# Three more chunks of the up projection by seven products, and more low parts of weights by DMA

## The chip, the cores and the metric

One core of one Trainium2 chip runs the whole program. The metric is device time in microseconds, the median of several runs. TensorE does the matmuls, VectorE (DVE) and ScalarE (ACT) the elementwise work, GpSimd (POOL) mostly issues DMAs that add into their destination, and SyncE (SP) issues the loads.

## The reference

A trunk of two residual layers over 512 tokens of width 1024, in float32. Layer 0 mixes tokens by gated linear attention, layer 1 by grouped-query softmax attention. After each mixer comes a gated MLP with a width-3 convolution over tokens:

```python
def conv_ffn(h, w_up, w_conv, b_conv, w_down):
    u = h @ w_up                      # 1024 -> 2 * 2816
    u = conv3(u, w_conv) + b_conv     # along tokens, per feature
    val, gate = jnp.split(u, 2, axis=-1)
    return (jax.nn.silu(gate) * val) @ w_down
for i in range(DEPTH):
    ...
    x = x + conv_ffn(rmsnorm(x, norm_ffn[i]), ffn_w_up[i], ffn_w_conv[i], ffn_b_conv[i], ffn_w_down[i])
```

The change touches the up projection of this MLP in both layers. (`conv3` stands for the reference's depthwise convolution.)

## The kernel before

**Two halves for one float32.** Every operand of a matmul is kept as a high part and a low part (`wh`, `wl` for weights; `nh`, `nl` and `xt` for activations), and a product is three matmuls: high by high, high by low, low by high. The high part is a copy by ScalarE that rounds. The low part is either a subtraction on VectorE (`split`, L320), or `low_dma`: ScalarE writes the negated rounded value (L272), and a DMA from POOL's queue (`flush`, L308) adds the unrounded value onto it, read from SBUF or, where `home` is given, from the weights in DRAM.

**Chunks.** The 2816 features of the MLP are 22 chunks `m` of 128, each with a value tile (t = 0) and a gate tile (t = 1) of 128 features x 512 tokens. There are two ways to compute a chunk:

- `plain_up(m)`: two tiles, each 8 steps of 3 matmuls with 512 columns, 48 matmuls (L482 to L484, output `up`). The weights are two pieces of 128 x 1024.
- `seven_up(m)`, for `m` in `SEVEN`: the two tiles by two halves of the tokens as a 2 x 2 block product, by seven block products in place of eight (the scheme of Strassen and Winograd). Each product has 4 pairs of 3 matmuls with 256 columns, 84 in all (L1074, output `r`). The weights are four pieces: two as loaded, a sum of quarters (h = 2, made with L293 and L294), and a half-size difference (h = 3). Between products ScalarE doubles a block (`twice`, L1129) or copies one (L1095, L1102), and VectorE adds (L1132); product 4 can only begin when the copy L1095 is done, product 6 when `twice` of product 1 is.

**Order.** `Weights.todo` is a list of the pieces in order of use; each call of `W.piece` makes pieces ahead of use (six in the wide phase from chunk 1 to 19, four after that) and loads three further ones through SP. Raw loads share a ring of five buffers of 128 x 1024 (`raw`), from which the sum tile is taken too; a buffer is free when the last reader of its contents has finished, a DMA included.

After chunk 9 and chunk 17 (`DOWN_AFTER`) a part of the down projection runs, four steps `n` of 84 narrow matmuls, again by seven products, each adding its result to x in DRAM through POOL's queue. Its first product is placed inside the chunk ahead (between the tiles of a plain chunk), as the first product of chunk m + 1 is placed inside a seven-product chunk m (`begin_up`), so that a doubling by ScalarE is covered by other matmuls. In `add_ffn` one swap in the list of pieces goes with it: the first piece of the down part comes ahead of the plain chunk's second piece.

Before, `SEVEN` holds 6, 7, 8, 10 to 13, 15, 16 and 18 to 21; chunks 0 to 5, 9, 14 and 17 are plain. `LOW_0`, `LOW_1` and `LOW_2` name the seven-product chunks whose piece h = 0, 1 or 2 gets its low part by DMA: chunks 7 and 8 for h = 0, none for the others. A piece h = 0 is read again from DRAM for that, a piece h = 2 from the sum tile in SBUF.

The engines' orders are not written by hand here: a scheduler orders each engine's instructions by priority and readiness at build time, and each engine then works through its list in order.

Of the kernel before, what the change touches and what calls it, by code (L numbers as in the profile page):

```python
# [66 lines left out]
DOWN_AFTER = {9: 0, 17: 1}  # L67


SEVEN = (6, 7, 8, 10, 11, 12, 13, 15, 16, 18, 19, 20, 21)  # L70
UPA = 3
PA = 4
LOADS = 3
# [1 line left out]
INPUT_AT = {2: (0, 1), 3: (2,), 4: (3,)}  # L75
Q_DMA = ()
UP_DMA = (1, 2, 5)
LOW_0 = (7, 8)
LOW_1 = ()
LOW_2 = ()  # L80
STRIP_0 = ()
STRIP_2 = ()
NR = 5
# [17 lines left out]
def hybrid_encoder_kernel(  # L101
# [39 lines left out]
    def bank(tag, n):  # L141
        return pp.tile([P, S], F32, tag=tag, bufs=PS[tag], name=nm(n))
# [4 lines left out]
    def big(dt, n):  # L147
        return pair("g", 22, dt, n)

    def tmp(tag, n, w=S):  # L150
        return sp.tile([P, w], F32, tag=tag, bufs={"u": 3, "t": 5, "sq": 3}[tag], name=nm(n))
# [24 lines left out]
    class Weights:  # L176
# [98 lines left out]
        def summed(self, src, i, h):  # L275
# [20 lines left out]
            r = self.strip[id(src), i][h]  # L296
            low = (LOW_0, LOW_1, LOW_2) if any(src is a for a in up) else (STRIP_0, (), STRIP_2)
            if i in low[h]:
# [41 lines left out]
    W = Weights()  # L340
# [3 lines left out]
    def add_up(layer, chunks):  # L344
        for m in chunks:
            W.add(up[layer], (m,), 4 if m in SEVEN else 2)
            if m in SEVEN and m - 1 not in SEVEN and m - 1 not in DOWN_AFTER:
                W.todo[-5:-3] = W.todo[-4], W.todo[-5]

    def add_ffn(layer):  # L350
        first = 0
        for m, part in DOWN_AFTER.items():
            add_up(layer, range(first, m + 1))
            W.add(down_w[layer], range(part * NQ, (part + 1) * NQ), 4)
            at = len(W.todo) - 4 * NQ - 1
            W.todo[at : at + 2] = W.todo[at + 1], W.todo[at]
            first = m + 1
        add_up(layer, range(first, FC))
        W.add(down_w[layer], range(NPART * NQ, down_w[layer].shape[0]))
# [9 lines left out]
    for a in qk_order[:2] + [w_av] + qk_order[2:] + [w_aout]:  # L369
        W.add(a)  # L370
    add_ffn(1)
    W.by_dma += [(w_kq, KQ_DMA)] + [(a, 1) for a in qk_order + [w_av]] + [(w_aout, 2)]

# [121 lines left out]
    def feature_tile(*a):  # L495
        for last in feature_steps(*a):
            pass
        return last
# [518 lines left out]
    def ffn(layer, norm, cw, nxt):  # L1017
        w_dn = down_w[layer]

        ahead = {(m + i // 2, i % 2): n for m in DOWN_AFTER for i, n in ((-1, 2), (0, 2), (1, 5))}  # L1020
        ahead.update({(m - 1 + i // 2, i % 2): n for m in SEVEN for i, n in ((-1, 2), (0, 2), (1, 5))})
        plain = {}
        down = []
# [5 lines left out]
        def rescale():  # L1029

            for p in range(KC // 2):
                xr = big(F32, "xr")
                for i in range(2):
                    c = 2 * p + i
                    dve.scalar_tensor_tensor(xr[:, i * S : (i + 1) * S], x[c], norm.weight(c), norm.R, ALU.mult, ALU.mult)
                hi, lo = big(F32R, "nh"), big(F32R, "nl")
                W.low_dma(hi, lo, xr)
                scaled.append(xr)
                fresh.extend((hi[:, i * S : (i + 1) * S], lo[:, i * S : (i + 1) * S]) for i in range(2))

        def plain_up(m):

            pss = []
            for t in range(2):
                ps = bank("s" if t else "acc", "up")
                feature_tile(*W.half(up[layer], 2 * m + t, max(UPAW if W.wide else UPA, ahead.get((m, t), 1))), norm.hl if m < SWITCH else fresh, ps)
                pss.append(ps)
                if t == 0 and m not in DOWN_AFTER:
                    begin_up(m + 1)
                if t == 0 and m in DOWN_AFTER:  # L1050
                    down.append(down_part(DOWN_AFTER[m], m))
                    next(down[-1])
                if m == 0 and t == 0:
                    norm.tokens()
                elif m == 0:
                    norm.rows()
                    rescale()
            for t, ps in enumerate(pss):
                u = ps
                if m < SWITCH:  # L1060
                    u = tmp("u", "u")
                    dve.tensor_tensor(u, ps, norm.R, ALU.mult)
                yield t, u

        def product(pieces, src, strip, pairs, i, dst, start):
            h, o = PLACE[i]
            if h not in pieces:
                pieces[h] = W.piece(src, strip, h, PAW if W.wide else PA)
            wh, wl = pieces[h]
            for j, p in enumerate(pairs):  # L1070
                sl = slice(o + j * P, o + (j + 1) * P)
                mh, ml = p[i]
                for a, (w, m) in enumerate(((wh, mh), (wh, ml), (wl, mh))):
                    mm(dst, w[:, sl], m, start=start and j == 0 and a == 0, stop=j == len(pairs) - 1 and a == 2,  # L1074
                       skip_group_check=True)
            W.flush()

        def begin_up(m):
            if m in SEVEN:
                begun.append(seven_up(m))  # L1080
                next(begun[-1])

        def seven_up(m):

            pieces = {}
            go = lambda *a: product(pieces, up[layer], m, inputs, *a)
            r = bank("pt", "r1")[:, :H]
            go(1, r, True)
            both = bank("acc", "r")
            r1, r2 = both[:, :H], both[:, H:]  # L1090
            twice(both, r)
            yield
            go(6, r2, False)
            r3 = bank("s", "r3")
            act.activation(r3[:, :H], r2, AF.Copy)  # L1095
            r4 = bank("pt", "r4")[:, :H]
            go(7, r4, True)
            d = tmp("u", "u")
            twice(d, r4)
            go(4, r3[:, :H], False)  # L1100
            go(5, r2, False)
            act.activation(r3[:, H:], r2, AF.Copy)  # L1102
            add_seven(d, r3, r4)
            yield 1, d
            begin_up(m + 1)
            go(2, r1, False)
            go(3, r2, False)
            yield 0, both

        def act_up(m):  # L1110

            res = {}
            for t, u in begun.pop(0) if m in SEVEN else plain_up(m):
                cc = ((layer * 2 + t) * FC + m) * 4
# [12 lines left out]
        def twice(d, r4):  # L1127
            two = lambda a: a.rearrange("p (o t) -> p o t", t=H)
            act.activation(two(d), two(r4).to_broadcast([P, 2, H]), AF.Copy)  # L1129

        def add_seven(d, r3, r4):
            dve.tensor_tensor(d, d, r3, ALU.add)  # L1132
# [49 lines left out]
        def down_part(part, m):  # L1182

            pairs = [quads.pop(part * NQ + i) for i in range(NQ)]
            st = {}
            pieces = [{} for _ in range(NQ)]
            go = lambda n, *a: product(pieces[n], w_dn, part * NQ + n, pairs, *a)

            def begin(n):
                r = bank("pt", "r1")[:, :H]
                go(n, 1, r, True)
                st[n] = bank("acc", "r")
                twice(st[n], r)

            begin(0)
            yield
            for n in range(NQ):
                r, c, d = st[n], x_home[n][:, :S], x_home[n][:, S:]  # L1200
                r1, r2 = r[:, :H], r[:, H:]
                go(n, 6, r2, False)
                r3 = bank("s", "r3")
                act.activation(r3[:, :H], r2, AF.Copy)
                r4 = bank("pt", "r4")[:, :H]
                go(n, 7, r4, True)
                g, f = tmp("u", "g"), tmp("u", "f")
                twice(f, r4)
                go(n, 4, r3[:, :H], False)
                go(n, 5, r2, False)  # L1210
                act.activation(r3[:, H:], r2, AF.Copy)  # L1211
                add_seven(f, r3, r4)
                W.pending.append((d, f))
                if n + 1 < NQ:
                    begin(n + 1)
                else:
                    begin_up(m + 1)
                go(n, 2, r1, False)
                go(n, 3, r2, False)
                act.activation(g, r, AF.Copy)  # L1220
                W.pending.append((c, g))
# [15 lines left out]
        for m in range(FC):  # L1237
# [15 lines left out]
            else:  # L1253
                for i, y in enumerate(held):
                    t = big(F32R, "gu")
# [244 lines left out]
    ffn(0, norms[1], cw, norms[2])  # L1500
    attention(norms[2], norms[3])
    ffn(1, norms[3], cw, None)


def _layout(inputs):
# [61 lines left out]
    seven = np.stack(quarters, 1).transpose(0, 4, 3, 1, 2, 5).reshape(2, FC, P, 4 * S)  # L1567
    a["w_up"][:, list(SEVEN)] = seven[:, list(SEVEN)]
    dn = i["ffn_w_down"].reshape(2, FC, P, KC, P)
# [29 lines left out]
```

## Time and profile before

| | |
|---|---|
| median of 3 runs | 1087.22 us (1086.87 to 1087.8) |
| profiled execution, span from first to last instruction | 1085.5 us |
| what lies around that span, against the runs' median | 1.7 us |
| TensorE busy | 1077.5 us, 99% |
| VectorE busy | 888.5 us, 82% |
| ScalarE busy | 721.1 us, 66% |
| GpSimd busy | 136.7 us, 13% |
| granted TensorE clock | 1.000 |

The span is one execution's time from its first to its last instruction. A busy share is a mean over stages. Matmuls overlap: the profile's length of one (0.39 us for 512 columns, 0.28 for 256) is longer than the distance from one to the next, so distances are taken from start times.

### The profile page before, as it was taken

To read this page: it belongs to the slowest core of one execution; us is meant where nothing else is said; L and a number is where in the kernel's file an instruction comes from. 1 tells how busy PE (TensorE), PEld (TensorE's weight loads), DVE (VectorE), ACT (ScalarE), POOL (GpSimd) and SP (SyncE) were. 2 spreads that over 40 slices of the span, in tenths; PEclk is the share of its full clock that TensorE was granted. 3 is DMA by queue.
4 is the path that set the end of the run, shared out by engine and by line. 5 is a ranking of instruction groups with operands and counts; after the bars stand their busy time and mean duration, and the time that the engine had idled before them with its cause. 6 is when DMAs were issued, how large, how long until landed. Compare 5 with 4: busy or idle time off the path is not lost.

```text
span 1085.5 us, 17391 instructions
## 1 busy us (share of the span) xinstructions
PE 1077.5 (99%) x6672; PEld 966.4 (89%) x6672; DVE 888.5 (82%) x1327; ACT 721.1 (66%) x1134; POOL 136.7 (13%) x153
## 2 busy tenths in 40 slices
PE   9999999999999999999999999999999999999998
PEld 8888988888999999999988888888889999999997
DVE  7998967569898899988755588666989889998882
ACT  8679575478775676666574677656877567666660
POOL 0212112021001100010015333002110010001000
PEclk9999999999999999999999999999999999999999
DMA  8744446499545633274767475549863473227542
GB/s 301 187 126 106 122 141 215 154 207 204 127 125 127 145 120 111 77 177 121 252 149 162 127 204 164 164 158 202 206 148 124 105 166 116 100 80 157 136 175 78
DMA packets 55763, 164.52 MB, mean 152 GB/s; under 512 B 6528, under 2 KB 7040, under 8 KB 55680
## 3 DMA queue, kind: packets, MB, share of 16 engines
q1 hardware_dynamic: 36192, 112.66, 32.2%
q0 software_dynamic: 14592, 42.21, 21.7%
q10 hardware_dynamic: 4896, 8.55, 2.1%
q8 instruction: 52, 0.85, 0.3%
q14 instruction: 31, 0.25, 0.1%
HBM read 114.89 MB, written 14.68 MB: 119 GB/s over the span
## 4 chain that ended last, share of the span: by engine, by line
PE 87%; DVE 6%; ACT 3%; DMA 2%; issue 2%; POOL 0%; SPq 0%; DVEq 0%; ACTq 0%; POOLq 0%
PE r L1074 37%; PE op L535 8%; PE vg L652 7%; PE up L482 4%; PE up L483 4%; PE up L484 4%; PE dn L483 2%; PE dn L484 2%; PE dn L482 2%; PE av L509 1%; PE A L482 1%; DVE wl L320 1%; PE A L484 1%; DMA nl<-xr 1%; PE B L484 1%
## 5 line engine op out<-in xcount | busy, mean ns | idle before, releaser
L320 DVE TENSOR_TENSOR wl<-raw,wh 128x1024 fp32r<-128x1024 f32 x156 | 189.8, 1220 | 31.3 <-ACT wh L319 31.1
L319 ACT ACTIVATE wh<-raw 128x1024 fp32r<-128x1024 f32 x156 | 162.6, 1053 | 73.4 <-PE op L535 20.7
L1074 PE MATMUL r<-gu,wh 128*128 128x256 f32 x896 | 161.2, 282 | 0.0
L1074 PE MATMUL r<-xt,wh 128*128 128x256 f32 x832 | 151.1, 283 | 0.4 <-ACT r L1095 0.3
L1074 PEld LDWEIGHTS r<-gu,wh 128*128 128x128 f32 x896 | 139.3, 190 | 1.0 <-ACT r L1211 0.2
L1074 PEld LDWEIGHTS r<-xt,wh 128*128 128x128 f32 x832 | 129.2, 190 | 1.6 <-ACT r L1095 1.1
L1074 PE MATMUL r<-gu,wl 128*128 128x256 f32 x448 | 126.3, 283 | 0.0
L1074 PE MATMUL r<-xt,wl 128*128 128x256 f32 x416 | 117.2, 283 | 0.0
L1074 PE MATMUL r<-nh,wh 128*128 128x256 f32 x312 | 88.8, 285 | 0.3 <-ACT r L1102 0.3
L1074 PE MATMUL r<-nh,wl 128*128 128x256 f32 x312 | 88.2, 283 | 0.0
L1074 PE MATMUL r<-nl,wh 128*128 128x256 f32 x312 | 87.9, 282 | 0.0
L1074 PEld LDWEIGHTS r<-gu,wl 128*128 128x128 f32 x448 | 85.1, 190 | 0.0
L1074 PEld LDWEIGHTS r<-xt,wl 128*128 128x128 f32 x416 | 79.1, 190 | 0.0
L482 PE MATMUL up<-nh,wh 128*128 128x512 f32 x192 | 75.3, 392 | 0.0
L483 PE MATMUL up<-nl,wh 128*128 128x512 f32 x192 | 75.2, 392 | 0.0
L484 PE MATMUL up<-nh,wl 128*128 128x512 f32 x192 | 75.2, 392 | 0.0
L535 PE MATMUL op<-oT,wh 128*128 128x512 f32 x256 | 72.4, 393 | 0.0
L271 ACT ACTIVATE wh<-raw 128x1024 fp32r<-128x1024 f32 x36 | 38.0, 1056 | 38.2 <-PE up L483 11.5
L1074 PEld LDWEIGHTS r<-nh,wh 128*128 128x128 f32 x312 | 59.3, 190 | 2.9 <-ACT r L1102 2.6
L1074 PEld LDWEIGHTS r<-nl,wh 128*128 128x128 f32 x312 | 59.4, 190 | 0.2
L1074 PEld LDWEIGHTS r<-nh,wl 128*128 128x128 f32 x312 | 59.4, 190 | 0.0
L535 PEld LDWEIGHTS op<-oT,wh 128*128 128x128 f32 x256 | 47.4, 188 | 9.7 <-ACT oT L937 0.3
(299 smaller groups left out, 2761.6 us busy)
## 6 DMA issues: line engine op xcount, KB each, us to landing
raw<-in_w_up_dram SPq DMA_DIRECT2D x84, 512.0 KB, 4.6
raw<-in_w_down_dram SPq DMA_DIRECT2D x44, 512.0 KB, 3.7
wl<-raw POOLq DMA_DIRECT2D x20, 512.0 KB, 5.3
wl<-in_w_up_dram POOLq DMA_DIRECT2D x16, 512.0 KB, 7.8
ring<-p ACTq DMA_DIRECT2D x32, 256.0 KB, 2.6
xw<-in_xw_dram SPq DMA_DIRECT2D x8, 512.0 KB, 6.6
raw<-in_w_v_dram SPq DMA_DIRECT2D x8, 512.0 KB, 5.9
raw<-in_w_g_dram SPq DMA_DIRECT2D x8, 512.0 KB, 4.0
```

What stands on the lines that cost most here:

```text
L271: act.activation(hi, r, AF.Copy)
L319: act.activation(hi[:, sl], a, AF.Copy)
L320: dve.tensor_tensor(lo[:, sl], a, hi[:, sl].bitcast(F32), ALU.subtract)
L482: mm(ps, wh, mh, start=start, stop=False)
L483: mm(ps, wh, ml, start=False, stop=False)
L484: return mm(ps, wl, mh, start=False, stop=stop)
L509: mm(ps[j][:, :width], hl[k][i == 2][:, j * P : (j + 1) * P], (wl if i == 1 else wh)[:, sl], start=k == 0 and i == 0, stop=k == KC - 1 and ...
L535: mm(pss[ng][n], wt[:, sl], mv, start=k == late[0][0] and i == 0, stop=k == late[-1][-1] and i == 2)
L652: last = mm(ps[j], m[:, js], w[:, sl], start=i in (1, 7, 2) and p == 0 and a == 0, stop=i in (4, 2, 3) and p == 3 and a == 2, skip_group_c ...
L1074: mm(dst, w[:, sl], m, start=start and j == 0 and a == 0, stop=j == len(pairs) - 1 and a == 2, skip_group_check=True)
```

## The change

`SEVEN` becomes all chunks from 6 to 21: chunks 9, 14 and 17 of both layers are computed by seven products. What follows a first product inside a chunk is chosen in one place, `begin(m)`: a down part where `m` is in `DOWN_AFTER`, otherwise the next chunk. The swap in `add_ffn` is kept for plain chunks alone. `LOW_0` gets 11 more chunks and `LOW_2` eight, so that 19 more pieces a layer get their low part by DMA. The weights of the three chunks are laid out as quarters on the host, which the existing code does from `SEVEN`.

```diff
-SEVEN = (6, 7, 8, 10, 11, 12, 13, 15, 16, 18, 19, 20, 21)
+SEVEN = tuple(range(6, 22))
...
-LOW_0 = (7, 8)
+LOW_0 = (7, 8, 9, 11, 12, 13, 14, 15, 16, 17, 19, 20, 21)
 LOW_1 = ()
-LOW_2 = ()
+LOW_2 = (8, 9, 13, 14, 15, 16, 17, 20)
...
             at = len(W.todo) - 4 * NQ - 1
-            W.todo[at : at + 2] = W.todo[at + 1], W.todo[at]
+            if m not in SEVEN:
+                W.todo[at : at + 2] = W.todo[at + 1], W.todo[at]
...
-                if t == 0 and m not in DOWN_AFTER:
-                    begin_up(m + 1)
-                if t == 0 and m in DOWN_AFTER:
-                    down.append(down_part(DOWN_AFTER[m], m))
-                    next(down[-1])
+                if t == 0:
+                    begin(m)
...
+        def begin(m):
+            if m in DOWN_AFTER:
+                down.append(down_part(DOWN_AFTER[m], m))
+                next(down[-1])
+            else:
+                begin_up(m + 1)
...
             yield 1, d
-            begin_up(m + 1)
+            begin(m)
             go(2, r1, False)
```

## The prediction

> **What bounds the kernel now.** I read the busy times of the engines first, then the chain that ended last, in order of time, then a table by stretch for the chunks that the change touches, and last single instructions there. The page's head:
>
> ```profile
> span 1085.5 us, 17391 instructions
> ...
> PE 1077.5 (99%) x6672; PEld 966.4 (89%) x6672; DVE 888.5 (82%) x1327; ACT 721.1 (66%) x1134; POOL 136.7 (13%) x153
> ```
>
> TensorE is busy for 99% of the span; POOL's 153 pieces of work take 0.89 us each. The chain in order of time (start, length, what) shows what TensorE spends a chunk on. Here it runs from chunk 8 through down part 0 and chunks 10 to 13 into plain chunk 14 of layer 0:
>
> ```profile
> 313.55 2.90 PE r L1074 x24
> ...
> 321.25 1.45 PE r L1074 x12
> ...
> 328.18 75.90 PE r L1074 x636
> 404.77 2.98 PE r L1074 x24
> ...
> 412.53 1.43 PE r L1074 x12
> ...
> 419.54 15.78 PE r L1074 x132
> ```
>
> L1074 is the matmul of 256 columns in a seven-product piece of work. 636 of them follow one another in 75.90 us without a wait, 0.1193 us each, so a seven-product chunk (7 products x 4 pairs x 3 = 84) takes 10.02 us. The rows between these, which I left out, are 512-wide matmuls of the plain chunks 9 and 14. From 313.55 to 328.18 are 14.63 us; the 24 and 12 narrow ones take 4.35, which leaves 10.28. From 404.77 to 419.54 are 14.77, less 4.41 leaves 10.36. In each of the two stretches lie 45 of the plain chunk's 48 matmuls (three stand ahead of it), so one costs 20.64/90 = 0.2293 us and a plain chunk 11.01 us.
>
> Now the same place by stretch. The columns are busy us (and counts) of TensorE, its weight loads, VectorE, ScalarE and GpSimd, then the granted clock, the share of the DMA engines and GB/s. The stretches are chunks 10 to 13, plain 14, 15 and 16, plain 17:
>
> ```profile
> core 0: us, PE busy (x) PEld busy (x) DVE busy (x) ACT busy (x) POOL busy (x), PEclk, DMA share, GB/s
> 368.10:408.20 40.10, 40.10 (x332) 39.71 (x331) 37.81 (x51) 28.24 (x44) 0.87 (x1) 1.00 0.46 127
> 408.20:419.40 11.20, 11.20 (x57) 9.39 (x56) 11.20 (x15) 6.86 (x10) 0.00 (x0) 1.00 0.33 111
> 419.40:439.50 20.10, 20.10 (x164) 19.73 (x163) 20.10 (x31) 14.52 (x24) 0.00 (x0) 1.00 0.32 105
> 439.50:450.50 11.00, 11.00 (x55) 9.27 (x54) 10.23 (x18) 7.48 (x12) 0.00 (x0) 1.00 0.16 48
> sum 82.40, PE 82.40 PEld 78.09 DVE 79.34 ACT 57.10 POOL 0.87; mean PE 20.60 PEld 19.52 DVE 19.84 ACT 14.27 POOL 0.22
> ```
>
> TensorE binds, but VectorE is full in chunks 14 to 16 (11.20 of 11.20, 20.10 of 20.10): the plain chunks are where it catches up. ScalarE has 25 us to spare, the DMA engines more than half.
>
> **The change, part by part.** *Matmuls.* In each of two layers chunks 9, 14 and 17 go from 48 wide to 84 narrow matmuls: 11.01 - 10.02 = 0.99 us less, six times 5.9 us. All of it is on the path.
>
> *Work around them.* The prices, from the groups by form (busy us, mean ns):
>
> ```profile
> L320 DVE TENSOR_TENSOR wl<-raw,wh 128x1024 fp32r<-128x1024 f32 x156 | 189.8, 1220 | 31.3 <-ACT wh L319 31.1
> L319 ACT ACTIVATE wh<-raw 128x1024 fp32r<-128x1024 f32 x156 | 162.6, 1053 | 73.4 <-PE op L535 20.7 <-DVE raw L294 14.4 <-PE dn L483 8.7
> ...
> L293 DVE TENSOR_TENSOR sum<-raw,raw 128x1024 f32<-128x1024 f32 x42 | 51.2, 1218 | 0.0
> ...
> L272 ACT ACTIVATE wl<-raw 128x1024 fp32r<-128x1024 f32 x36 | 37.7, 1047 | 0.2 <-PE op L535 0.2
> ...
> L286 DVE TENSOR_TENSOR wl<-raw,wh 128x512 fp32r<-128x512 f32 x42 | 28.9, 688 | 17.7 <-PE r L1074 17.6
> ...
> L285 ACT ACTIVATE wh<-raw 128x512 fp32r<-128x512 f32 x42 | 26.3, 627 | 7.9 <-DVE raw L283 7.7
> ...
> L1129 ACT ACTIVATE r<-r 128x512 f32<-128x512 f32 x42 | 24.4, 580 | 15.9 <-PE r L1074 15.7
> ```
>
> A seven-product chunk needs on VectorE one more low part (1.22), the sum (1.22), two half-tile differences, a half low part and an add (4 x 0.69): 5.2 us more than a plain one. On ScalarE it needs one more high part (1.05), a half one (0.63), two doublings (2 x 0.58) and two copies of 0.37: 3.6 us more. It loads the same two 512 KB halves, so SP's queue gets no load more, but the sum takes a third buffer of the five for raw weights.
>
> *Low parts by DMA.* Each of the 19 takes 1.22 us from VectorE, gives ScalarE 1.05 (L272), POOL's queue one issue of 0.89, and the DMA engines one more transfer of 512 KB that adds into SBUF. Per layer VectorE has 3 x 5.2 - 19 x 1.22 = -7.6 us, ScalarE 3 x 3.6 + 19 x 1.05 = +30.8, POOL +16.9. Twelve of the 19 lie in chunks 11 to 17. There VectorE goes from 79.3 of 82.4 us to 79.3 + 10.4 - 14.6 = 75.1 of 80.4: a little better than now, so its cover holds. ScalarE goes from 57.1 to 57.1 + 7.2 + 12.6 = 76.9 of 80.4: from 69% to 96%, or some 92%, since neighbours overlap by 0.1 (the 2.00 below for two halves). That engine loses its cover, and the next question is who waits for it.
>
> Its tightest duty is the quarter copy L1095 between two products, here in chunk 12, with TensorE's start of products 6, 7 and 4:
>
> ```profile
> 380.20 1.06 ACT L319 ACTIVATE wh<-sum 128x1024 fp32r<-128x1024 f32 x1
> ...
> 381.70 2.00 ACT L319 ACTIVATE wh<-raw 128x1024 fp32r<-128x1024 f32 x2
> ...
> 389.87 0.37 ACT L1095 ACTIVATE r<-r 128x256 f32<-128x256 f32 x1 [0.72 <-PE r L1074]
> ```
> ```profile
> 388.17 0.40 PE L1074 MATMUL r<-xt,wh 128*128 128x256 f32 x2
> ...
> 389.61 0.39 PE L1074 MATMUL r<-xt,wh 128*128 128x256 f32 x2
> ...
> 391.04 0.40 PE L1074 MATMUL r<-xt,wh 128*128 128x256 f32 x2
> ```
>
> The copy comes as early as it can (ScalarE sat idle for it) and ends at 390.24, 0.80 us ahead of product 4 at 391.04. One weight half of 1.05 in front of it costs at most 0.25 us, two (2.00) cost 1.2. Chunk 8 of layer 1 shows the loss once:
>
> ```profile
> 828.53 0.37 ACT L1095 ACTIVATE r<-r 128x256 f32<-128x256 f32 x1
> ```
> ```profile
> 828.95 0.39 PE L1074 MATMUL r<-xt,wh 128*128 128x256 f32 x1 [0.34 <-ACT r L1095]
> ```
>
> The second duty is the landing. Chunk 12's third piece has its high part at 381.26; with 0.95 for the negated copy the transfer can start at 382.2, and product 7 wants it at 389.61: 7.4 us. The first piece of chunk 13 is done at 383.70, its copy at 384.65, and product 1 wants it four products after 388.17, at 388.17 + 48 x 0.1193 = 393.9: 9.2 us. The rows for such transfers: the median over the whole run, from the page's list of DMA issues; then the same list for 230 to 265 us, where the two queues take 90% of the DMA engines:
>
> ```profile
> wl<-raw POOLq DMA_DIRECT2D x20, 512.0 KB, 5.3
> ```
> ```profile
> q0 software_dynamic: 1170, 4.27, 65.7%
> q1 hardware_dynamic: 725, 2.63, 24.7%
> ...
> raw<-in_w_up_dram SPq DMA_DIRECT2D x6, 512.0 KB, 5.7
> nl<-xr POOLq DMA_DIRECT2D x4, 512.0 KB, 7.6
> wl<-in_w_up_dram POOLq DMA_DIRECT2D x3, 512.0 KB, 8.2
> ```
>
> POOL's queue moved 4.27 MB there (8.1 transfers) in 65.7% of 35 us, 2.8 us of all engines each. Chunks 10 to 17 now have 0.46 x 40.1 + 0.33 x 11.2 + 0.32 x 20.1 + 0.16 x 11.0 = 30.3 us of such time; twelve more transfers make 64 of 80.4, 80%, and more in 13 to 17, which have two each. So the third piece has between 7.4 - 5.3 = 2.1 us to spare and 0.2 too few; the first piece between 3.9 and 1.0, or 0.9 too few if its raw load is also slower, 5.7 in place of the median of 3.8 that SP's loads take in chunks 10 to 13:
>
> ```profile
> DMA to landing us min/median/max: 3.5/3.8/7.0
> ```
>
> [...]
>
> What all this costs TensorE: 16 chunks (8, 9, 13 to 17 and 20, in two layers) get two low parts by DMA. At best nothing is late (0); at worst each is 0.9 late (14.4 us). The spare times are nearer to the good end, so I take one high part's length (1.05) at one chunk in eight: 2.1 us.
>
> *Chunks 7 to 9.* These follow the busiest stretch, and ScalarE gets there chunk 9's extra 3.6 and three low parts. At best the 0.34 wait above goes (its weight came late); at worst chunks 8 and 9 wait for one more half each in both layers, 4 x 1.05 = 4.2. I take 0.3, nearest the one wait shown.
>
> *Order.* Down parts 0 and 1 now begin inside seven-product chunks, as the next chunk's first product does already in 10 to 13; the swap of two pieces goes because the order of use does. Where a part begins, TensorE meets the same cover (24 narrow matmuls, 2.9 us) for the doubling of 0.58: nothing. POOL's issues stand behind the additions to x in one queue, but no such addition is due from chunk 10 to 17 (0.87 us of POOL in 82.4), so nothing for them either, and the cost if that failed is a late landing as above.
>
> Sum: -5.9 + 2.1 + 0.3 = -3.5, a span of 1082.0. The median of the runs, 1087.22, is 1.7 above the profiled span; so 1083.7.
>
> **The rivals.** *All kept.* Nothing is late and the old wait goes unused: 1087.2 - 5.9 = 1081.3. For it: 0.80, 2.1 and 3.9 us of spare. Against: ScalarE at 92 to 96%.
> *Landings late.* With 0.4 us lost at each of the 16 chunks, 6.4 against 5.9: 1087.7, no change. For it: the crowded rows; against: they come from a stretch where four transfers wait in one burst. At the full 0.9 it is 1095.7.
> *ScalarE binds.* In the same 16 chunks the copy L1095 stands behind two halves: 1.2 us late. At half of them 9.6 - 5.9 = +3.7: 1090.9, slower. It breaks even at 5.9/16 = 0.37 us a chunk, and is slower beyond 0.51. For it: the one wait shown came at a lower load than 96%; against: in chunk 12 ScalarE idles right before the copy.
> *Narrow matmuls don't pay.* It would need over 11.01/84 = 0.131 us for one; the row has 0.119. At 0.14 each the six chunks would add 4.5 us: 1091.7. [...]
>
> **How the numbers follow.** A difference of 0.2% (2.2 us) is about what a measurement of this kernel tells from none. The forecast, 1082.2 to 1085.0, gets 0.38; all kept 0.22; landings late with no change 0.20, and beyond it 0.06; ScalarE binds 0.12; narrow matmuls 0.02. Faster is 0.38 + 0.22 = 0.60, same 0.20, slower 0.20. The range runs from all kept with the old wait gone as well (1087.2 - 5.9 - 0.3, rounded down: 1080.8) to the upper end of no change, 1089.4, and leaves out the slower cases.
>
> **What would show it.** Right: no 512-wide matmuls of up after chunk 5; one run of L1074 from chunk 6 to the end of 21 at 0.1193 to 0.1200 us each; VectorE below 100% in chunks 14 to 16; ScalarE above 85% there. Wrong: waits of TensorE for the copy (ACT r) or for a transfer into wl in chunks 8, 9 and 13 to 17; transfers of wl that take over 8 us. A layer would have 24 pieces of 84 narrow matmuls (16 chunks, 8 steps of the down parts), 4032 in all, so a mean of 0.1208 (5.9/4032 more) eats the gain.

## The result, and the profile after

The changed kernel takes 1144.24 us (median of 4 runs, 1143.55 to 1145.05) against 1087.05 us for the kernel before (4 runs of the same session): a ratio of 1.053, 95% interval 1.051 to 1.054. The forecast was 1083.7. The profiled spans are 1141.8 and 1085.5 us: 56.3 us came, where 3.5 were to go. Below, one run of `pinned` (1758.92 us) and one of `c9_17l` (2134.12 us) lie far above the others of their kernel and are left out of its time and its ratio.

The page of the changed kernel, its head and the shares of the chain that ended last:

```profile
span 1141.8 us, 18050 instructions
...
PE 1095.5 (96%) x6888; PEld 990.3 (87%) x6888; DVE 882.8 (77%) x1325; ACT 772.5 (68%) x1208; POOL 169.8 (15%) x191
...
PE 77%; ACT 8%; DVE 6%; issue 5%; DMA 4%; POOL 0%; SPq 0%; ACTq 0%; POOLq 0%; DVEq 0%
```

TensorE was 99% busy and is 96% busy, while no other engine became full. In the line numbers of the changed kernel the narrow matmul is L1072, the copies of the first and second half of r3 are L1100 and L1107, `twice` is L1134. What TensorE waited for longest (us in total, times, longest):

```profile
PE r L1072 <- DMA wl<-sum: 15.5, 8, 4.2
PE r L1072 <- ACT r L1107: 13.4, 6, 2.5
PE r L1072 <- ACT u L1134: 7.6, 8, 2.8
```

The added copies, from the groups by form (38 more than before: 58 - 36, and 16):

```profile
L272 ACT ACTIVATE wl<-raw 128x1024 fp32r<-128x1024 f32 x58 | 60.7, 1047 | 0.2 <-PE op L536 0.2
...
L272 ACT ACTIVATE wl<-sum 128x1024 fp32r<-128x1024 f32 x16 | 16.7, 1044 | 0.0
```

The chunks between the two down parts (10 to 17) of layers 0 and 1, first before, then after; columns as in the prediction's table. Each stretch ends where the first product of down part 1 starts: after half of plain chunk 17 before, after five of its seven products after. In matmuls the two are nearly the same length: 492 narrow and 72 wide ones (75.2 us at 0.1193 and 0.2293 us) before, 636 narrow ones (75.9 us) after.

```profile
368.28:443.63 75.35, 75.35 (x566) 71.97 (x565) 73.16 (x101) 52.82 (x81) 0.87 (x1) 1.00 0.40 118
887.54:962.77 75.23, 75.23 (x566) 72.00 (x565) 72.75 (x101) 52.75 (x81) 0.86 (x1) 1.00 0.37 113
```
```profile
373.75:464.61 90.86, 81.04 (x634) 79.09 (x633) 73.81 (x105) 68.14 (x104) 10.42 (x12) 0.96 0.68 159
916.95:1017.72 100.77, 85.40 (x629) 83.56 (x629) 75.10 (x108) 69.73 (x105) 10.39 (x12) 0.90 0.63 145
```

These two stretches hold 15.5 + 25.5 = 41 of the 56 us. ScalarE has 68 to 70 us of work in 91 and 101, so it is idle for a quarter to a third of the time, while TensorE waits for it. The granted clock, 1.00 before, is 0.96 and 0.90.

The starts of the matmuls in the two narrow regions give nearly the whole sum. Gaps of more than 0.3 us between neighbouring narrow ones hold 43.3 us (above 0.119 each) after and 0.7 before: +42.6. Another 191 neighbours stand 0.20 to 0.225 us apart in place of 0.119 (9 before): +17.3, matmuls at half the clock (granted clock 0.50 in 948.60 to 952.80, the longest row of them). The matmuls' own time is 5.6 less (504 more narrow ones at 0.120 us, 288 fewer wide ones at 0.2295). Together +54.3 of the 56.3; the rest was not traced.

### The profile page after: what moved, and what is told of

Same layout as the page of the kernel before. It is cut to its first block, busy times and chain, and to the rows that moved or that the text cites. A ratio compares the mean times of both kernels' runs of the same rounds, so it can differ in the third digit from the quotient of the medians.

```text
span 1141.8 us, 18050 instructions
## 1 busy us (share of the span) xinstructions
PE 1095.5 (96%) x6888; PEld 990.3 (87%) x6888; DVE 882.8 (77%) x1325; ACT 772.5 (68%) x1208; POOL 169.8 (15%) x191
## 4 chain that ended last, share of the span: by engine, by line
PE 77%; ACT 8%; DVE 6%; issue 5%; DMA 4%; POOL 0%; SPq 0%; ACTq 0%; POOLq 0%; DVEq 0%
PE r L1072 30%; PE op L536 8%; PE vg L653 7%; PE up L483 4%; PE up L484 4%; PE up L485 4%; DMA wl<-sum 3%; PE dn L483 2%; PE dn L485 2%; PE dn L484 2%; ACT wl L272 2%; DVE sum L293 1%; ACT wh L271 1%; PE av L510 1%; ACT wh L319 1%
## 5 line engine op out<-in xcount | busy, mean ns | idle before, releaser
L1072 PE MATMUL r<-xt,wh 128*128 128x256 f32 x1024 | 191.2, 285 | 7.9 <-ACT u L1134 7.6
L320 DVE TENSOR_TENSOR wl<-raw,wh 128x1024 fp32r<-128x1024 f32 x134 | 163.1, 1220 | 36.5 <-ACT wh L319 36.3
L319 ACT ACTIVATE wh<-raw 128x1024 fp32r<-128x1024 f32 x134 | 140.5, 1052 | 61.7 <-PE op L536 20.7
L1072 PEld LDWEIGHTS r<-xt,wh 128*128 128x128 f32 x1024 | 160.1, 191 | 11.2 <-ACT u L1134 9.2
L1072 PE MATMUL r<-gu,wh 128*128 128x256 f32 x896 | 162.5, 283 | 0.2
L1072 PE MATMUL r<-xt,wl 128*128 128x256 f32 x512 | 144.3, 286 | 15.5 <-DMA wl<-sum 15.5
L1072 PEld LDWEIGHTS r<-gu,wh 128*128 128x128 f32 x896 | 139.0, 190 | 1.4 <-ACT r L1216 0.5
L1072 PE MATMUL r<-nh,wh 128*128 128x256 f32 x384 | 117.0, 305 | 13.5 <-ACT r L1107 13.4
L1072 PE MATMUL r<-gu,wl 128*128 128x256 f32 x448 | 126.1, 283 | 0.0
L1072 PE MATMUL r<-nh,wl 128*128 128x256 f32 x384 | 114.8, 299 | 0.4 <-DMA wl<-in_w_up_dram 0.4
L1072 PE MATMUL r<-nl,wh 128*128 128x256 f32 x384 | 115.0, 299 | 0.0
L1072 PEld LDWEIGHTS r<-xt,wl 128*128 128x128 f32 x512 | 97.4, 192 | 17.3 <-DMA wl<-sum 17.1
L1072 PEld LDWEIGHTS r<-nh,wh 128*128 128x128 f32 x384 | 80.0, 208 | 16.3 <-ACT r L1107 16.0
L1072 PEld LDWEIGHTS r<-gu,wl 128*128 128x128 f32 x448 | 85.1, 190 | 0.0
L1072 PEld LDWEIGHTS r<-nh,wl 128*128 128x128 f32 x384 | 80.1, 208 | 0.6 <-DMA wl<-in_w_up_dram 0.6
L1072 PEld LDWEIGHTS r<-nl,wh 128*128 128x128 f32 x384 | 80.3, 209 | 0.1
L308 POOL DMA_DIRECT2D wl<-in_w_up_dram x38 | 33.2, 872 | 238.7 <-ACT wl L272 157.1
L286 DVE TENSOR_TENSOR wl<-raw,wh 128x512 fp32r<-128x512 f32 x48 | 33.2, 691 | 37.2 <-PE r L1072 37.2
L272 ACT ACTIVATE wl<-raw 128x1024 fp32r<-128x1024 f32 x58 | 60.7, 1047 | 0.2 <-PE op L536 0.2
```

What stands on the lines that cost most here:

```text
L272: act.activation(lo, r, AF.Copy, scale=-1.0)
L286: self.last = dve.tensor_tensor(lo, r, hi.bitcast(F32), ALU.subtract)
L308: pool.dma_start(lo.bitcast(F32) if same else lo, r, accum_op=ALU.add)
L319: act.activation(hi[:, sl], a, AF.Copy)
L320: dve.tensor_tensor(lo[:, sl], a, hi[:, sl].bitcast(F32), ALU.subtract)
```

## The experiments

Each run's ratio is against the kernel before, timed on the same chip in the same session. "Narrow region" is the time from the first to the last narrow matmul of a layer; before it takes 251.3 and 253.1 us.

### Each part of the change alone

`seven_only` keeps the seven products and takes back the low parts; `low_only` puts the new lists into the kernel before, where chunks 9, 14 and 17 are plain, so that 13 pieces a layer get a low part by DMA.

```diff
 seven_only: changed kernel with
-LOW_0 = (7, 8, 9, 11, 12, 13, 14, 15, 16, 17, 19, 20, 21)
-LOW_2 = (8, 9, 13, 14, 15, 16, 17, 20)
+LOW_0 = (7, 8)
+LOW_2 = ()
```

> Chunks 9, 14 and 17 by seven products and the down parts inside them as in the changed kernel, LOW_0 and LOW_2 as before. Order theory (the added low parts make the planner put part of product 7 of the next chunk ahead of products 2 and 3 of this one on TensorE, and TensorE then waits for ScalarE and for landings): only 6 of some 28 such displacements are left here, so 1082 to 1092 us. Load theory (ScalarE and the DMA engines are full in chunks 13 to 17): both are as free as before, so 1081 to 1086, or up to 1095 if VectorE, which gets 10 us more in chunks 10 to 17, becomes late. Chunk theory (the seven-product form where the down parts begin is what costs): 1125 or more.

> The kernel before with the new LOW_0 and LOW_2 alone; chunks 9, 14 and 17 stay plain, so 13 low parts a layer are added rather than 19 (LOW_0 for 11, 12, 13, 15, 16, 19, 20, 21, LOW_2 for 8, 13, 15, 16, 20). Order theory: the displaced products are there in about 16 places, so 1110 to 1130 us. Load theory: ScalarE reaches some 85% in chunks 10 to 17 instead of 96%, the DMA engines 70%, so 1087 to 1100. Chunk theory: 1085 to 1090, no change.

`seven_only`: 1102.07, ratio 1.014 [1.012, 1.015]. `low_only`: 1112.0, ratio 1.023 [1.021, 1.025]. Neither part pays; `seven_only` is slower than the order and load theories allowed and faster than the chunk theory. 15 and 25 us leave some 17 of the 57 to the 12 copies that `low_only` lacks and to the meeting of the two. They wait for different things, `seven_only` for high and low parts of weights that VectorE's late sum holds back (the profile puts both down to L319):

```profile
PE r L1072 <- ACT wh L319: 9.4, 10, 2.6
```
```profile
367.25:447.00 79.75, 76.82 (x637) 76.09 (x636) 77.71 (x107) 56.15 (x88) 0.87 (x1) 1.00 0.35 102
```

The second row is its chunks 10 to 17: VectorE is busy for 77.71 us there, more than the 75.9 that the stretch's 636 matmuls need. The three plain chunks were its time to catch up, as the prediction had read. `low_only` waits for the new transfers and for the copies of r3 (L1102 and L1095 as before):

```profile
PE r L1074 <- DMA wl<-sum: 9.5, 5, 3.0
PE r L1074 <- ACT r L1102: 3.6, 3, 1.9
```

### TensorE's order

In the changed kernel the scheduler put 2 to 12 matmuls of the next chunk's product 7 ahead of this chunk's products 2 and 3, at 28 places (3 before). `pinned` keeps products 6 and 7 behind product 3 of the chunk before; `pinned_seven_only` and `pinned_before` do the same to their namesakes.

```diff
-go(6, r2, False)
+with tc.issue_after(closing[-1].ins): go(6, r2, False)     # also go(7, ...)
...
-go(3, r2, False)
+closing.append(go(3, r2, False))
```

> The changed kernel with TensorE's order fixed: products 6 and 7 of a chunk (and of a step of a down part) are queued behind product 3 of the chunk before. Same work, same low parts. Order theory: most of the 57 us come back, 1082 to 1092. Load theory: TensorE waits for the same late copies and landings in another order, 1125 to 1150. Chunk theory: 1130 to 1150.

> The three chunks by seven products with the old LOW lists, and TensorE's order fixed as in the pinned kernel. Order theory: 1080 to 1086, as the last displacements go too. Load theory: the same as the unpinned one within 2 us. Chunk theory: 1125 or more.

> The kernel before with the same pin of products 6 and 7 behind product 3 of the chunk before. A control: the pin itself is worth nothing where TensorE lost 3.5 us in both regions: 1083 to 1088 by every theory.

`pinned`: 1133.48, ratio 1.043 [1.041, 1.045] (the expectations below call it 1134.1); `pinned_seven_only`: 1103.4, 1.015 [1.013, 1.016]; `pinned_before`: 1087.52, 1.000 [0.9995, 1.0014]. The order is some 11 of the 57 us, the pin itself costs nothing, and the order theory falls for the rest. What the pin does is clear the view: most of the 42.8 us in gaps now has one name, the copy of r3's second half (L1110 here):

```profile
PE r L1072 <- ACT r L1110: 33.8, 22, 3.8
```

### Copy or transfer

Both runs start from `pinned`. `p_nocopy` leaves out ScalarE's negated copy of the 38 added low parts and lets the DMA write instead of add; `p_nodma` keeps the copies and leaves out the DMAs.

```diff
 p_nocopy, for the added low parts
 act.activation(hi, r, AF.Copy)
-act.activation(lo, r, AF.Copy, scale=-1.0)
-pool.dma_start(lo, r, accum_op=ALU.add)
+pool.dma_start(lo, r)
```

> The pinned kernel (TensorE's order kept regular, 1134.1 us), in which ScalarE leaves out the negated copy of the nineteen added low parts of a layer and GpSimd's DMA writes the piece itself instead of adding it to the copy: the transfers and their issue stay, 1.2 us of ScalarE a piece goes (the values of these low parts are wrong by it). Queue theory (the second half's copy of r3 stands in ScalarE's queue behind the copies that the low parts added): 1085 to 1105, most of the 34 us of TensorE's waits for that copy go. Landing theory (the low parts arrive late, or the transfers crowd the DMA engines): 1125 to 1136. Chunk theory (the seven form in the chunks 7, 9, 14 and 17 costs by itself): no lower than the 1103 of the pinned kernel with the old low parts.

> The pinned kernel, in which ScalarE keeps the negated copies of the nineteen added low parts of a layer, but their DMAs are left out (the low parts are wrong by it). Queue theory: 1125 to 1136, the waits of TensorE for the second half's copy of r3 stay at 28 to 34 us. Landing theory: 1085 to 1105.

`p_nocopy`: 1091.44, ratio 1.004 [1.003, 1.005]; `p_nodma`: 1133.0, 1.042 [1.040, 1.044]. Without the copies 42 us go; without the transfers 0.5, which is inside the spread of the four runs (1130.8 to 1135.7). Against `pinned_seven_only` (1103.4), which has the old low parts, the 38 moved ones cost 30 us with their copies and give 12 without them. TensorE's waits for the second half's copy, in that order:

```profile
PE r L1079 <- ACT r L1117: 6.8, 9, 1.3
```
```profile
PE r L1075 <- ACT r L1113: 33.8, 22, 3.8
```

38 copies of 1.05 us are 39.8 us of ScalarE; on an engine that is a third idle their removal gives more than their length. Two readings show how. First the kernel before, chunk 12, ScalarE from product 4 on, and TensorE's start of product 2, which needs the copy L1102:

```profile
391.24 0.60 ACT L1129 ACTIVATE u<-r 128x512 f32<-128x512 f32 x1 [0.32 <-PE r L1074]
391.73 1.05 ACT L319 ACTIVATE wh<-sum 128x1024 fp32r<-128x1024 f32 x1
392.68 2.00 ACT L319 ACTIVATE wh<-raw 128x1024 fp32r<-128x1024 f32 x2
394.57 0.38 ACT L1102 ACTIVATE r<-r 128x256 f32<-128x256 f32 x1
```
```profile
395.32 0.28 PE L1074 MATMUL r<-nh,wh 128*128 128x256 f32 x1
```

Product 5 ends near 393.9, product 1 of the next chunk runs until 395.3, and the copy is done at 394.95: 0.37 us to spare, behind a block of three weight copies. Now `pinned`, layer 1, the same place and one chunk on:

```profile
947.27 0.60 ACT L1137 ACTIVATE u<-r 128x512 f32<-128x512 f32 x1 [1.07 <-PE r L1072]
947.77 1.05 ACT L319 ACTIVATE wh<-raw 128x1024 fp32r<-128x1024 f32 x1
948.72 1.05 ACT L271 ACTIVATE wh<-sum 128x1024 fp32r<-128x1024 f32 x1
949.66 1.05 ACT L272 ACTIVATE wl<-sum 128x1024 fp32r<-128x1024 f32 x1
950.61 1.05 ACT L271 ACTIVATE wh<-raw 128x1024 fp32r<-128x1024 f32 x1
951.56 0.62 ACT L285 ACTIVATE wh<-raw 128x512 fp32r<-128x512 f32 x1
952.08 1.04 ACT L272 ACTIVATE wl<-raw 128x1024 fp32r<-128x1024 f32 x1
953.02 0.37 ACT L1110 ACTIVATE r<-r 128x256 f32<-128x256 f32 x1
...
967.11 0.37 ACT L1110 ACTIVATE r<-r 128x256 f32<-128x256 f32 x1
...
968.23 0.81 ACT L1125 ACTIVATE y<-u,cw 128x512 f32<-128x512 f32 x1 [0.28 <-DVE u L1140]
970.70 0.63 ACT L1129 ACTIVATE y<-y 128x512 f32<-128x512 f32 x1 [1.67 <-DVE y L1127]
973.05 0.78 ACT L1125 ACTIVATE y<-r,cw 128x512 f32<-128x512 f32 x1 [1.72 <-PE r L1072]
974.83 0.37 ACT L1102 ACTIVATE r<-r 128x256 f32<-128x256 f32 x1 [1.00 <-PE r L1072]
```
```profile
951.23 0.28 PE L1072 MATMUL r<-nh,wl 128*128 128x256 f32 x1
953.44 0.39 PE L1072 MATMUL r<-nh,wh 128*128 128x256 f32 x1 [1.93 <-ACT r L1110]
...
967.53 0.58 PE L1072 MATMUL r<-nh,wh 128*128 128x256 f32 x1 [3.80 <-ACT r L1110]
967.90 0.41 PE L1072 MATMUL r<-nl,wh 128*128 128x256 f32 x1
968.12 0.41 PE L1072 MATMUL r<-nh,wl 128*128 128x256 f32 x1
```

The block is 5.25 us (947.77 to 953.02) where it was 2.84, and TensorE stands still until the copy is through. The next block, ahead of the wait of 3.80 us, is 7.1 us (959.99 to 967.11): six weight copies and four copies for the down projection's input (L1146). Right after being late (967.11) ScalarE idles 0.28 + 1.67 + 1.72 + 1.00 us: the first two for VectorE's steps that follow the late copy, the other two for TensorE's products 3 and 6, which that copy had held back. Two of VectorE's steps close what is called the ring below:

```profile
972.84 0.69 DVE L286 TENSOR_TENSOR wl<-raw,wh 128x512 fp32r<-128x512 f32 x1 [2.23 <-PE r L1072]
973.45 1.22 DVE L293 TENSOR_TENSOR sum<-raw,raw 128x1024 f32<-128x1024 f32 x1
```

L286 writes the low part of a strip's last piece; its buffers (`sq`, three for two tiles a strip) come free with product 3. The sum L293 is queued behind L286 by a rule in `summed`, and ScalarE's block holds the copies of that sum and of the piece made with it. So: product 3, L286, sum, block of copies, copy of the second half, product 2, product 3. In `pinned` this wait of L286 is plain between the down parts of layer 1 (6.9 us in five waits) and hardly there in layer 0 (0.4 us in one); nor did L286 wait ahead of the 7.1 us block (956.49), so not every long block is the ring's.

### Moving the copies, moving the victim

`p_late0` (from `pinned`) holds both ScalarE copies of each first piece with a low part by DMA back until the second half's copy is queued. `p_r3dve` (from `pinned`) lets VectorE make that copy.

```diff
 p_late0
-act.activation(hi, r, AF.Copy); act.activation(lo, r, AF.Copy, scale=-1.0)
+self.held.append((hi, lo, r, home))        # both copies traced right behind act.activation(r3[:, H:], r2)
 p_r3dve
-act.activation(r3[:, H:], r2, AF.Copy)
+dve.tensor_copy(r3[:, H:], r2)
```

> The pinned kernel (1134.1 us) with one thing moved: ScalarE's two copies (the rounded one and the negated one) of each first piece with a low part by DMA, 2.2 us, are queued behind the second half's copy of r3 instead of ahead of it. The same copies and DMAs, the same total on every engine. Slot theory (between the two halves' copies of r3 TensorE has three products, 4.3 us, and ScalarE's queue in it was full before the change, so that each added copy delays the second half's copy by its whole length): 1100 to 1115, and TensorE's waits for that copy fall from 33.8 us to 10 or less; the third pieces' copies stay in the slot. Load theory (ScalarE's total is what costs): 1128 to 1138.

> The pinned kernel, in which VectorE writes the second half of r3 from product 5, instead of ScalarE (up and down parts). VectorE's next step in that chain is the sum that reads it. Queue theory: the copy no longer stands behind ScalarE's weight copies, 20 to 30 of the 34 us of waits go: 1100 to 1115; what is left is VectorE's own queue and the copies for the first half and for twice r, which stay on ScalarE. Landing theory and chunk theory: 1128 to 1138, as the copy would only be the place where another lateness shows.

`p_late0`: 1130.67, ratio 1.040 [1.038, 1.042]. The waits for the second half's copy fell almost as the slot theory had it (11.8 us, from 33.8), the time did not; it lies where the load theory had it:

```profile
PE r L1083 <- DMA wl<-in_w_up_dram: 16.7, 7, 3.8
PE r L1083 <- ACT r L1122: 11.8, 10, 2.8
PE r L1083 <- DMA wl<-sum: 6.0, 5, 2.1
```

A copy ahead of the second half's delays TensorE; the same copy behind it lands its low part too late. Room in one slot is not enough. `p_r3dve`: 1167.15, ratio 1.072 [1.071, 1.074], 52 us above its range: the copy now stands in VectorE's queue, behind low parts (L320) and the steps that prepare the down projection, and TensorE waits for it there:

```profile
PE r L1072 <- DVE r L1110: 40.3, 17, 6.2
```

### Cutting the ring

`p_free` (from `pinned`) drops the rule that queues the sum behind L286. `p_sq4` (from `pinned`) keeps the rule and gives `sq` a fourth buffer, at the cost of one of five `t` buffers. `b_free` drops the rule in the kernel before.

```diff
 p_free, b_free
-with tc.issue_after(self.last.ins) if self.last else ExitStack():
+with ExitStack():
     dve.tensor_tensor(both(e), ..., ALU.subtract)
 p_sq4
-bufs={"u": 3, "t": 5, "sq": 3}
+bufs={"u": 3, "t": 4, "sq": 4}
```

> The pinned kernel (1134.1 us) without one queueing rule that stands in both kernels: VectorE's sum for the third piece of a strip (line 293) is no longer queued behind the last low part of the strip before (line 286), which itself waits for product 3 of the running chunk. All copies, DMAs and sums stay. Loop theory (product 3 -> line 286 -> sum -> ScalarE's copies in one block -> second half's copy of r3 -> product 2 -> product 3: ScalarE idles before the block and is late after it, so each added copy lengthens the loop): 1090 to 1112, and the waits for that copy fall from 33.8 us to 12 or less. Load theory (ScalarE's total is what costs, wherever it stands): 1125 to 1140.

> The pinned kernel with a fourth buffer for the last pieces of a strip (taken from the five of the y tiles, which keep four), the queueing rule kept: line 286 no longer waits for product 3 of the running chunk. Loop theory: the loop is cut at another place, 1090 to 1115, unless the missing y buffer makes a wait of its own. Load theory: 1125 to 1140.

> A control: the kernel before without the same queueing rule. There the block of copies fits between the two halves' copies, so the loop doesn't bind: 1084 to 1092 by both theories.

`p_free`: 1108.39, ratio 1.019 [1.018, 1.021]. `p_sq4`: 1108.43, 1.020 [1.018, 1.021]. `b_free`: 1095.73, 1.008 [1.006, 1.009], slower than either theory allowed. Cut at either of two places, with every copy, sum and transfer kept, the kernel loses 25 us, as the loop theory said and the load theory did not. In the profiled executions the narrow regions went from 264.1 + 285.4 us to 264.2 + 266.9 in `p_free` (an execution of 1114.6 us, its slowest) and to 255.6 + 263.3 in `p_sq4`, which lost 8 us ahead of layer 0's region, where it has one `t` buffer fewer. So most of the gain is in layer 1, where the ring showed. Waits for the second half's copy, `p_free` (12 or less were expected) then `p_sq4`:

```profile
PE r L1072 <- ACT r L1110: 18.5, 10, 4.8
```
```profile
PE r L1072 <- ACT r L1110: 7.8, 12, 2.0
```

The traces also show what the cuts changed in ScalarE's queue. Between the two halves' copies of r3 stand, in the mean over a kernel's seven-product chunks, 2.2 copies of weights in the kernel before, 4.5 in `pinned`, 2.1 in `p_free` and 2.3 in `p_sq4`. With the sum no longer behind that wait, the scheduler spread the same copies over the chunk. So the cuts confirm that the block ahead of that copy costs, and that the rule and the shared buffers pack it; how much of the 25 us is lateness that feeds itself while the kernel runs, and how much is the queue's new order, these runs do not separate.

In the kernel before the rule is worth 8.7 us (`b_free`); why was not traced.

### What a version that pays looks like

`c9` is the kernel before with chunk 9 by seven products, `c9t` the same with one count set (which third wide piece goes into an `x` buffer, as in the kernel before). `c9_17` adds chunk 17, `c9_17l` also sets the count and adds two low parts a layer. `few` is `pinned` with the count set and five added low parts a layer.

```diff
 c9, c9t
+SEVEN = tuple(m for m in range(6, 22) if m not in (14, 17))
 c9t, c9_17l, few
+W.loads, W.wide, W.turn = LOADS_FFN, 1, layer
 c9_17, c9_17l
+SEVEN = tuple(m for m in range(6, 22) if m != 14)
 c9_17l
+LOW_0 = (7, 8, 15, 16)
 few
+LOW_0 = (7, 8, 12, 13, 14, 15, 16)      # LOW_2 = () in all five, LOW_0 = (7, 8) in the others
```

> The kernel before with chunk 9 alone by seven products and down part 0 begun inside it; chunks 14 and 17 stay plain and the low parts are those of before. Chunk theory (the form, or a part begun inside such a chunk, costs by itself): 1088 or more. VectorE theory (the 15 us that the three chunks cost together with the old low parts came from chunks 14 and 17, where VectorE has no time left; a plain chunk was its time to catch up): chunk 9 keeps its 2 x 1.0 us: 1084 to 1086.5.

> As the run with chunk 9 alone, with chunk 17 by seven products as well and down part 1 begun inside it; only chunk 14 stays plain. VectorE theory: down part 1 starts with VectorE behind, and some of the waits seen there come: 1084 to 1092. Chunk theory: 1092 or more.

> Chunk 9 alone by seven products (1091.6 us), with one number set: the count by which every third wide piece goes into a free x buffer starts at 1 in the second layer, as in the kernel before; chunk 9's extra piece had moved it to 2. In the run without this the two regions of the narrow products took 3.3 us less than before, and one wait of 3.6 us for a low part by DMA stood in the second layer's plain chunks, ahead of the region. If that wait hangs on the count: 1083 to 1085. If chunk 9 by seven costs there by itself: 1090 to 1092.

> Chunks 9 and 17 by seven products (chunk 14 plain), with only two more low parts a layer by DMA, those of the first pieces of the chunks 15 and 16, and the count set as in the run with chunk 9 alone. In the run with chunks 9 and 17 and the old low parts the narrow region lost 2.2 us a layer at the start of down part 1 to low parts late from VectorE. Loop theory: one negated copy in two chunks fits ahead of the second half's copy of r3 (product 1 of the next chunk covers 1.4 us) and gives VectorE 2.4 us back: 1082 to 1086. Load theory: 1087 to 1090.

> The pinned kernel with all chunks by seven, and with five added low parts a layer instead of nineteen: the first pieces of the chunks 12 to 16 (no third pieces, and the count set). Loop theory: one negated copy a chunk is 1.0 us in a block that had 0.6 us and product 1 to spare, so little of it shows, and VectorE gets 6 us a layer back: 1090 to 1101, below the 1103 of the same kernel without them. Load theory: 1103 to 1112, each copy a loss.

| run | us | ratio to before |
|---|---|---|
| c9 | 1091.55 | 1.004 [1.002, 1.005] |
| c9t | 1086.82 | 1.000 [0.999, 1.001] |
| c9_17 | 1087.59 | 1.000 [0.999, 1.001] |
| c9_17l | 1085.20 | 0.998 [0.997, 0.999] |
| few | 1095.95 | 1.008 [1.007, 1.010] |

`c9` contradicts the expectation by its time and not by its place: the narrow regions took 250.9 + 250.3 us, 3.3 less than before, and one wait of 3.6 us stood in layer 1's plain chunks. Setting the count took that wait away; `c9t` is 4.7 faster than `c9`, though short of the 1083 to 1085 expected. So chunk 9 by seven, with down part 0 begun inside it, does not cost by itself, nor does it give its 2 us. `few` is 7 us below the kernel without its five low parts (`pinned_seven_only`, 1103.4), as the loop theory said. It differs from that kernel by the count too, but only in layer 1; layer 0's narrow region, where the count is the same, fell from 259.4 to 255.3 us. One negated copy a chunk mostly fits, and VectorE is relieved: 75.2 us of work in chunks 10 to 17 of layer 0, 77.7 in `seven_only`. `c9_17l` is faster than before by 0.18%, near the least that can be told, and is the one version here that beats both kernels; against `c9_17` its narrow region is 2.9 us shorter in layer 0 and 1.5 longer in layer 1.

## Why the prediction was wrong, point by point

- **Matmuls, -5.9: held.** 0.119 us a narrow matmul, 5.6 us less of matmul time in the two narrow regions.
- **VectorE's cover holds: held.** With the low parts moved it had 73.8 us of work in the first stretch of 90.9, and it bound nothing by its total; without them (`seven_only`) it did. ScalarE's load was near the forecast 92% too: 68.1 us, 90% of the 75.9 that the matmuls need, though 75% of the 90.9 that the stretch took.
- **"That engine loses its cover, and the next question is who waits for it": the step that failed.** The prediction named the copy of r3's first half (L1095, 0.80 us to spare) as ScalarE's tightest duty. The tighter one was the second half's copy, L1102, with 0.37 us, 4.7 us further down the same timeline; a queued copy adds 0.95 (947.77 to 948.72 in `pinned` above). By this estimate the copy is 1.5 us late in each of 14 chunks that get two more copies and 0.6 in each of 10 that get one: 14 x 1.5 + 10 x 0.6 = 27 us, enough to make the rival "ScalarE binds" the forecast, though at another copy than the one it names. Measured, the copies are worth 42 us (`p_nocopy`), and 33.8 us of `pinned`'s waits are for L1102's copy.
- **The pieces' places taken as fixed.** Spare times were worked out as if a piece were made at the same moment as before. It hung on product 3 through L286 and the sum, and its copies moved with it into the block ahead of L1102. In the kernel before, VectorE came to L286 after product 3 in chunks 10 to 17 (0.2 us of waits in each layer), so the ring did not bind there; after the change it waits 7.1 and 7.5 us in them. Its wait for product 3 in the whole run, before and after:

```profile
DVE wl L286 <- PE r L1074: 17.6, 13, 2.3
```
```profile
DVE wl L286 <- PE r L1072: 37.2, 30, 2.4
```
- **Late lows, +2.1: the transfers were not slower than allowed.** By the page's list the median one took 4.5 us from the sum and 7.2 from DRAM, within the 5.3 to 8.2 of the prediction or below it. The 15.5 us of waits for `wl<-sum` in the changed kernel come from transfers that start late: the wait that ends at 306.31 is for one whose sum began at 298.17, whose copy ended at 301.43, and which was issued at 301.7 and landed 4.5 us later. In `pinned`, where TensorE waits for the copy anyway, leaving out all 38 transfers gives no more than the spread (`p_nodma`). What they would cost with the copies out of the way is not shown; `p_sq4` waits 6.6 us for low parts from DRAM.
- **Order, "nothing": wrong by some 11 us.** The scheduler moved parts of product 7 forward, at places that the change never named.
- **Chunks 7 to 9, +0.3: wrong, and outside its bound of 4.2.** Four waits there (1.2 and 2.1 us that end at 306.31 and 319.24, 2.4 and 2.5 at 846.81 and 860.88) hold 8.2 us, two for a transfer from the sum and two for the second half's copy, the same kinds as in the later chunks. `c9t` shows that chunk 9's form is not the reason.
- **A wait priced at its own length: wrong.** 17.3 of the 56.3 us are matmuls at half the clock after waits (below). No term stood for that.

Not settled: what the ring does not explain. `p_free` and `p_sq4` are still 21 us slower than before, with VectorE at 70.4 and ScalarE at 68.4 of 82.6 us in the first stretch of `p_free`; its 636 matmuls would have to follow one another in 75.9 us for the change to pay in full, which leaves VectorE 5.5 and ScalarE 7.5 us. What holds layer 0 back in `pinned`, where L286 hardly waits between the down parts, was not traced. A ring cut in both places at once was not run, nor a fourth `sq` buffer in the kernel before.

## What to carry to other kernels

ScalarE worked through its list in order: in `pinned` product 5 ended near 949.9, and the copy that needs it began at 953.02, behind six weight copies. Spare time of such an engine is worth what its tightest consumer leaves: list every short copy that another engine waits for, take the one with the least slack in the timeline, and price each added instruction ahead of it at its full length beyond that slack (here a block of 5.25 us in place of 2.84, a slack of 0.37 and a wait of 1.93). Then ask whether the added work's own input depends on that consumer; if it does, the work can come in a block right ahead of it (4.5 weight copies between the two halves' copies in `pinned`, 2.1 in `p_free`), and idle time elsewhere in the chunk does not help (ScalarE had 68.1 us of work in 90.9). Here five moved pieces a layer gave 7 us (`few`) where nineteen cost 30 (`pinned`), each against the same kernel with the old low parts.

## What the runs showed of the hardware

TensorE's clock fell after some waits. In `pinned`, with the wait of 3.80 us shown above, the matmuls that follow start 0.213 us apart, not 0.119, and the granted clock of that stretch is 0.50:

```profile
967.50:972.80 5.30, 5.27 (x24) 0.50 0.69 138
```

Full speed was back at 973.7, after 6.2 us: from there on the matmuls start 0.12 us apart again. In the changed kernel ten stretches of 14 to 21 matmuls ran so, 3.0 to 4.4 us long, at a granted clock of 0.50 (861.00 to 864.20 and 948.60 to 952.80 are two of them); the waits ahead of them lasted 2.1 to 4.4 us, while another of 2.1 us and all below 1.6 us had none behind them. The wait of 2.1 us that ends at 1082.61 had one; behind the other, which ends at 319.24, the clock was 1.00 for the next 3.06 us. Nor did it fall in `pinned` from 391.20 to 404.40, where TensorE was busy for 10.30 of 13.20 us: 1.00 there too. So the length of the wait alone did not decide it; what else did, no run here shows.
